# q and k of an attention unit: one transfer each over 128 partitions in place of two halves of 64

## The chip, the core and the metric

The kernel runs on one core of a Trainium2 chip. The metric is device time in microseconds for one execution of the whole program. The profile names the engines PE (matmul), PEld (weight load of the matmul engine), DVE (vector), ACT (scalar), POOL (GpSimd) and SP (the engine that mostly issues transfers). The core has 16 DMA engines, which move the data of every transfer, whichever engine issues it.

## What is computed

A decoder block with two parallel token mixers over 2048 positions of width 1024, batch 1. One combined projection gives q, k and v for 24 heads of 64 in three groups, gates, and the input of a recurrent branch. The attention branch is the part that matters here:

```python
for g, (window, dilation) in enumerate(((128, 1), (512, 4), (2048, 16))):
    o_g, lse_g = dilated_band_attention(q[:, :, g], k[:, :, g], v[:, :, g], window, dilation)
    outs.append(o_g)
    lses.append(lse_g)
wts = jax.nn.softmax(jnp.stack(lses, axis=0), axis=0)
attn = jnp.sum(wts[..., None] * jnp.stack(outs, axis=0), axis=0)
y_a = (attn.reshape(B, S, ATTN_OUT_WIDTH) * jax.nn.silu(g_attn)) @ w_attn_proj
...
merged = gates[:, :, 0] * y_a + gates[:, :, 1] * y_b
x = layer_norm(DEEPNORM_ALPHA * x + merged @ w_out + b_out, ln_gain, ln_bias)
```

Each query block of 128 sees its own key block and the one before it, along a residue class of the dilation.

## The kernel before

The program has three stages, one behind the other on PE, each engine working through a list that is fixed when the program is built.

**The projection** (L639) fills the first two thirds of the time. Its results go to DRAM: q and k after the rotary embedding into `qk_scr`, one buffer of 128 rows by 2048 float32 for each unit, v into `v_scr`, the rest into other scratch buffers. A row of `qk_scr` holds one head dimension of one of the unit's two heads, and rows of the two heads alternate.

**Attention** works on 12 units, each a pair of heads of one group. A unit has 16 query blocks and is done in four groups of the loop over `G`, 48 groups in all. In a group PE makes the scores of four blocks (`scores`, L992 and L998), turns the probabilities (`turn_p`, L1029), multiplies by v (`values`, L1061), and, from the fourth group on, does a piece of the second branch's output projection (`yb_part`, L1231). The scores of a unit read the tile `AT_X["qk", u % 2]`, 128 partitions by 2 by 2048: index 0 of the middle axis is q, 1 is k. Head 0 of the pair lies on partitions 0 to 63, head 1 on 64 to 127. There are two such tiles, so unit u + 1 is loaded while unit u is worked on, into the tile that unit u - 1 has left.

**The tail** does the rest of `yb`, the output projections and the layer norm.

The loads that the change touches are issued on SP's queue. `qk_parts(u)` (L791) gives a list of functions, each of which issues one load. Those of units 0 and 1 are called at steps 1 and 5 of the last pass of the projection (`begin`). For the others the loop at L1304 puts them into groups: the loads of q of unit u + 1 are issued in group 4u, the first group of unit u, those of k in group 4u + 1:

```python
for u in range(1, 11):
    for i, fn in enumerate(qk_parts(u + 1)):
        at_group(4 * u + i // 2, fn)
    for i, fn in enumerate(v_parts(u + 1)):
        at_group(4 * u + 1 + i // 2, fn)
```

Beside them SP issues, in the same stretch and in an order fixed by the code: the weights of `yb` (`wlr`, L1181), its inputs (`hx`, L1202), its gates (`gB`, L1215) and results (`yb_scr`, L1242), v (`V`, L815 to L819), and the softmax statistics (`ml_scr`, `mt`, L1085 to L1101; `wh`, L1148). Transfers issued on SP take eight completion semaphores in turn (DMAHW0 to DMAHW7 in the rows below), and each waits until the transfer eight places ahead of it, which had the same semaphore, has landed.

Of the kernel before, what the change touches and what calls it, by code (L numbers as in the profile page):

```python
# [31 lines left out]
def hybrid_block_kernel(ctx: ExitStack, tc: tile.TileContext, a: dict, out: bass.AP):  # L32
    nc = tc.nc
    sp, act, dve, pool, pe = nc.sync, nc.scalar, nc.vector, nc.gpsimd, nc.tensor
# [17 lines left out]
    qk_scr = {(n, u): dram.tile([P, S], F32, name=f"{n}_scr{u}") for u in range(12) for n in ("q", "k")}  # L52
# [53 lines left out]
    def big(slot, shape, dt, name):  # L106
        return (cur["Z"] if slot[0] == "Z" else X).tile(shape, dt, name=name, tag=slot)
# [203 lines left out]
    lo_, up_ = slice(0, 64), slice(64, P)  # L311
# [248 lines left out]
    qk = [("qk", FT_K + u, FT_Q + u) for u in range(12)]  # L560
# [152 lines left out]
    for s, pl in enumerate(plan):  # L713
        if pl[0] and pl[4] == "ug":
            i = pl[1][1][0] - FT_U
# [68 lines left out]
    AT_X = {}  # L784
    UG = {0: 0, 2: 1, 1: 2}

    def unit(u):

        return (0, 2, 1)[u % 3], u // 3

    def qk_parts(u):  # L791

        g, hp = unit(u)

        def part(x, h, hs):
            def fn():
                if u < 2 and (x, h) == (0, 0):
                    AT_X["qk", u] = big(("X2", "X3")[u], [P, 2, S], F32, f"qk{u}")
                src = qk_scr["qk"[x], 4 * g + hp].rearrange("(d h) s -> h d s", h=2)
                sp.dma_start(AT_X["qk", u % 2][hs, x], src[h])  # L800
            return fn

        return [part(x, h, hs) for x in range(2) for h, hs in ((0, lo_), (1, up_))]

    def v_parts(u):
        g, hp = unit(u)
        src = v_scr[g][hp]

        def part(i):
            def fn():  # L810
                if u == 0 and i == 0:
                    AT_X["v"] = big("X4", [P, 2, 16, P], F32, "V")
                V = AT_X["v"][:, u % 2, 4 * i:4 * i + 4]
                if g == 0:
                    sp.dma_start(V, src.rearrange("(p n) f -> p n f", p=P)[:, 4 * i:4 * i + 4])  # L815
                elif g == 1:
                    sp.dma_start(V, src[i * CH:(i + 1) * CH].rearrange("(j r) f -> j r f", r=4))
                else:
                    sp.dma_start(V, src.rearrange("(i r) f -> i r f", r=16)[:, 4 * i:4 * i + 4])  # L819
            return fn  # L820

        return [part(i) for i in range(4)]
# [48 lines left out]
    for t in sorted(early):  # L871
        for fn in early[t]:
            at(max(t, 0), fn)

    begin = {1: qk_parts(0), 3: v_parts(0), 5: qk_parts(1)}
    low = NS
    where = [(s, j) for s in range(NQ) for j in range(ticks[s])]
# [401 lines left out]
    def at_group(g, fn):  # L1279
        todo.setdefault(g, []).append(fn)  # L1280
# [22 lines left out]
        at_group((1, 1, 2, 2, 3, 3, 4, 4)[k], lambda k=k: split_h(k))  # L1303
    for u in range(1, 11):  # L1304
        for i, fn in enumerate(qk_parts(u + 1)):
            at_group(4 * u + i // 2, fn)
        for i, fn in enumerate(v_parts(u + 1)):
            at_group(4 * u + 1 + i // 2, fn)
    WS = {}
# [19 lines left out]
    for hp in range(3):  # L1329
        e = 4 * (3 * hp + 2) + 4  # L1330
        for i in range(12):
            c, g = i // 3, (0, 2, 1)[i % 3]
# [328 lines left out]
```

## Time and profile before

| | |
|---|---|
| median of 3 runs | 2112.81 us (2111.79 to 2115.16) |
| span of the profiled execution, first to last instruction | 2110.6 us |
| median of the runs less that span | 2.2 us |
| first and last matmul of scores start at | 1451.15 and 1764.4 us |
| loads of q and k | 48 of 512 KB |
| moved in the whole execution | 443.10 MB |

The profiled execution gives its span alone; what lies around it is taken as the 2.2 us in the table. In the profile a tile's name stands without its number, so `qk` is both tiles. Rows of a timeline give the start, the duration, the engine (with q where only its instruction queue is meant), the line, the operation with out<-in, and how many such instructions are merged. For a transfer the duration is that of issuing it, not of moving the data.

### The profile page before, as it was taken

Reading aid. Unit: us, or ns where it says so; the run is one execution under the profiler, and the core shown is the slowest. Engines: PE = TensorE matmul, PEld = TensorE weight load, DVE = VectorE, ACT = ScalarE, POOL = GpSimd, SP = SyncE. Lnnn points to the kernel's source line nnn. Section 1 sums busy time; section 2 is a strip of 40 time slices with the busy share of each in tenths; the row PEclk is TensorE's granted clock in tenths of the full one; section 3 lists DMA queues with packets and bytes.
Section 4 is the critical chain, followed back from the end, with each engine's and each line's share of the span. In section 5 each row is a group of like instructions: output and inputs, shape, how many; then the busy total and the mean of one; then the engine's idle time right before and its main releaser. Section 6 shows DMA issues by size and latency. Waiting matters only on the chain.

```text
span 2110.6 us, 35731 instructions
## 1 busy us (share of the span) xinstructions
PE 2092.4 (99%) x12069; PEld 1713.1 (81%) x12069; DVE 1645.0 (78%) x2937; ACT 1212.7 (57%) x2510; POOL 764.2 (36%) x685
## 2 busy tenths in 40 slices
PE   9999999999999999999999999999999999999998
PEld 7888888888888888888888888887888878788886
DVE  8878988989988868677777878875667776877667
ACT  6456556567567556677677787775666664321100
POOL 1544653653653301111111111112547678521120
PEclk9999999999999999999999999999999999999999
DMA  7876976886886866566665666669879886774431
GB/s 222 245 230 196 266 227 203 255 239 208 248 256 210 301 192 181 191 205 174 206 190 175 207 205 204 188 205 275 209 208 260 233 234 184 243 243 154 152 100 70
DMA packets 259205, 443.10 MB, mean 210 GB/s; under 512 B 65504, under 2 KB 92160, under 8 KB 255952
## 3 DMA queue, kind: packets, MB, share of 16 engines
q1 hardware_dynamic: 242384, 408.38, 62.0%
q0 software_dynamic: 11744, 23.54, 6.0%
q10 hardware_dynamic: 4896, 8.92, 1.1%
q8 instruction: 96, 1.57, 0.3%
q14 instruction: 85, 0.70, 0.1%
HBM read 289.74 MB, written 150.99 MB: 209 GB/s over the span
## 4 chain that ended last, share of the span: by engine, by line
PE 95%; DMA 2%; DVE 1%; POOL 1%; ACT 1%; issue 1%; SPq 0%; ACTq 0%; POOLq 0%; DVEq 0%
PE q L639 65%; PE yb L1231 6%; PE o L1061 3%; PE z L1536 3%; PE z L1537 3%; PE z L1538 3%; PE pt L1029 2%; PE s L998 2%; PE ya L1504 1%; PE ya L1503 1%; PE ya L1505 1%; PE g L500 1%; PE vtp L370 1%; PE s L992 1%; DMA war<-in_w_f_dram 1%
## 5 line engine op out<-in xcount | busy, mean ns | idle before, releaser
L639 PE MATMUL q<-xT,hS 128*128 128x512 f32 x1632 | 505.0, 391 | 0.1
L639 PE MATMUL q<-xT,l 128*128 128x512 f32 x1088 | 423.5, 389 | 0.0
L639 PE MATMUL q<-xB,hA 128*128 128x512 f32 x1344 | 418.0, 392 | 0.0
L639 PE MATMUL q<-xB,l 128*128 128x512 f32 x944 | 367.9, 390 | 0.0
L639 PEld LDWEIGHTS q<-xT,hS 128*128 128x128 f32 x1632 | 304.6, 188 | 65.0 <-issue 2.7
L639 PEld LDWEIGHTS q<-xB,hA 128*128 128x128 f32 x1344 | 250.7, 188 | 57.0 <-issue 5.8
L639 PEld LDWEIGHTS q<-xT,l 128*128 128x128 f32 x1088 | 204.3, 188 | 42.6
L240 POOL TENSOR_TENSOR sw<-sw,sin 128x512 f32<-128x512 f32 x96 | 156.8, 1639 | 166.2 <-ACT sw L329 94.7
L639 PEld LDWEIGHTS q<-xB,l 128*128 128x128 f32 x944 | 177.5, 188 | 37.2
L240 POOL TENSOR_TENSOR y<-y,h 128x512 f32<-128x512 f32 x28 | 38.8, 1386 | 384.1 <-DVE h L541 352.1
L1014 ACT ACTIVATE pb<-pb 128x192 f32<-128x192 f32 (+1 forms) x384 | 160.7, 422 | 26.5 <-DVE pb L1012 26.4
L639 PE MATMUL q<-xB,hS 128*128 128x512 f32 x544 | 169.0, 392 | 0.0
L639 PE MATMUL q<-xT,hA 128*128 128x512 f32 x544 | 167.8, 390 | 0.0
L284 ACT ACTIVATE hA<-wA 128x512 fp32r<-128x512 f32 x220 | 138.6, 636 | 28.5 <-DVE l L240 9.1
L1231 PE MATMUL yb<-hx,wl 128*128 128x512 f32 x576 | 148.9, 400 | 0.1
L284 ACT ACTIVATE hS<-S 128x512 fp32r<-128x512 f32 x170 | 108.6, 639 | 60.7 <-DVE S L240 47.3
L240 POOL TENSOR_TENSOR l<-wA,hA 128x512 fp32r<-128x512 f32 x68 | 107.8, 1585 | 91.4 <-ACT hA L284 60.9
L1231 PEld LDWEIGHTS yb<-hx,wl 128*128 128x128 f32 x576 | 104.8, 188 | 28.4 <-issue 5.6
L639 PEld LDWEIGHTS q<-xT,hA 128*128 128x128 f32 x544 | 101.9, 188 | 21.4 <-issue 0.4
L639 PEld LDWEIGHTS q<-xB,hS 128*128 128x128 f32 x544 | 101.2, 188 | 21.5 <-issue 1.1
L240 DVE TENSOR_TENSOR S<-S,wA 128x512 f32<-128x512 f32 x102 | 96.8, 949 | 11.5 <-DMA wA<-in_w_in_dram 7.9
L1507 POOL TENSOR_TENSOR me<-gA,me 128x512 f32<-128x512 f32 x30 | 47.7, 1607 | 157.6 <-DVE gA L1506 135.3
(213 smaller groups left out, 4325.4 us busy)
## 6 DMA issues: line engine op xcount, KB each, us to landing
wA<-in_w_in_dram SPq DMA_DIRECT2D x220, 256.0 KB
wl_scr<-l SPq DMA_DIRECT2D x102, 512.0 KB
l<-wl_scr SPq DMA_DIRECT2D x102, 512.0 KB
wS<-in_w_in_dram SPq DMA_DIRECT2D x102, 256.0 KB
wS<-in_w_in_dram POOLq DMA_DIRECT2D x68, 256.0 KB, 7.0
wlr<-in_w_f_dram SPq DMA_DIRECT2D x64, 256.0 KB
mg_scr<-y SPq DMA_DIRECT2D x59, 256.0 KB
v_scr<-vs SPq DMA_DIRECT2D x48, 256.0 KB
```

The source lines that it names most:

```text
L240: eng.tensor_tensor(out=out, in0=in0, in1=in1, op=op)
L284: act.activation(heads(h), heads(r, False), AF.Copy)
L639: pe.matmul(bank, w[:, ks], x[:, kk, xx], start=(first and i == 0), stop=(last and i == 11))
L998: pe.matmul(bank[h][es, b, 0:BW], q[hs, n * P + 64 * e:n * P + 64 * e + 64], k_[hs, at + 64 * e:at + 64 * e + BW], start=True, stop=True)
L1014: act.activation(pp, pp, AF.Exp, scale=-1.0, bias=mm, accum_out=ll)
L1029: pe.transpose(pt[e][:, b, 2 * h + x, :], pdata(p, h, c, c + P)[hs], ident[hs, hs])
L1061: pe.matmul(o[hs, 2 * i + b, :], V[:, kb, 64 * h:64 * h + 64], ptb[:, b, 2 * h + x, :], start=(x == lo // P), stop=(x == 1))
L1231: pe.matmul(YB["t"], w[:, a, k], hx(8 * c + k)[:, b], start=(hf == 0 and m == 0), stop=(hf == 1 and m == 11))
L1507: (dve if i in (6, 7) else pool).tensor_tensor(out=ME[c][:, f], in0=ga, in1=ME[c][:, f], op=ALU.add)
L1536: pe.matmul(z, mh[:, k], w[:, 0, hs], start=(k == 0), stop=False)
L1537: pe.matmul(z, mh[:, k], w[:, 1, hs], start=False, stop=False)
L1538: pe.matmul(z, ml[:, k], w[:, 0, hs], start=False, stop=(k == 7))
```

## The change

The list of `qk_parts` has two functions in place of four. Each issues one load whose destination is all 128 partitions of q or of k, and whose source is the whole buffer, seen as head, dimension, position. The view of the source is the one that was there before; it was cut at its first axis before and is passed whole now. The list being half as long, the loop's `i // 2` becomes `i`.

```diff
-        def part(x, h, hs):
+        def part(x):
             def fn():
-                if u < 2 and (x, h) == (0, 0):
+                if u < 2 and x == 0:
                     AT_X["qk", u] = big(("X2", "X3")[u], [P, 2, S], F32, f"qk{u}")
-                src = qk_scr["qk"[x], 4 * g + hp].rearrange("(d h) s -> h d s", h=2)
-                sp.dma_start(AT_X["qk", u % 2][hs, x], src[h])
+                sp.dma_start(AT_X["qk", u % 2][:, x], qk_scr["qk"[x], 4 * g + hp].rearrange("(d h) s -> h d s", h=2))
             return fn
 
-        return [part(x, h, hs) for x in range(2) for h, hs in ((0, lo_), (1, up_))]
+        return [part(x) for x in range(2)]
...
         for i, fn in enumerate(qk_parts(u + 1)):
-            at_group(4 * u + i // 2, fn)
+            at_group(4 * u + i, fn)
```

SP's list at the end of the projection, before: the loads of units 0 and 1, with v of unit 0 between them, and behind them the first weights and inputs of `yb`. A row gives the line, the operation, out<-in, the shape of the destination and a count.

```order
L800 DMA qk_13859<-q_scr_90 64x2048 x2
L800 DMA qk_13859<-k_scr_91 64x2048 x2
L815 DMA V<-v_scr_78 128x512 x4
L800 DMA qk_13937<-q_scr_106 64x2048 x2
L800 DMA qk_13937<-k_scr_107 64x2048 x2
L1181 DMA wlr_14029<-in_w_f_dram 128x512
L1181 DMA wlr_14030<-in_w_f_dram 128x512
L1202 DMA hx_13980<-hb_scr 128x512 x4
```

The same place in the changed program, here with the semaphores that each row waits for:

```order
L799 DMA qk_13859<-q_scr_90 128x1x2048 [waits DMAHW5_49,PE_49]
L799 DMA qk_13859<-k_scr_91 128x1x2048 [waits DMAHW6_49]
L814 DMA V<-v_scr_78 128x512 [waits DMAHW7_49,PE_49]
L814 DMA V<-v_scr_78 128x512 [waits DMAHW0_49]
L814 DMA V<-v_scr_78 128x512 [waits DMAHW1_49]
L814 DMA V<-v_scr_78 128x512 [waits DMAHW2_49]
L799 DMA qk_13935<-q_scr_106 128x1x2048 [waits DMAHW3_49]
L799 DMA qk_13935<-k_scr_107 128x1x2048 [waits DMAHW4_49]
L1180 DMA wlr_14025<-in_w_f_dram 128x512 [waits DMAHW5_49,PE_49]
L1180 DMA wlr_14026<-in_w_f_dram 128x512 [waits DMAHW6_49,Pool_49]
```

Eight rows of 64x2048 have become four of 128x1x2048; nothing else has changed its place, and the eight semaphores are reached again four transfers later. The first `wlr` now waits for the semaphore of the first load of q, the second for that of k.

The same inside attention, from the load of q of unit 3 to that of unit 4, before:

```order
L800 DMA qk_13937<-q_scr_92 64x2048 x2
L1181 DMA wlr_14852<-in_w_f_dram 128x512
L1181 DMA wlr_14853<-in_w_f_dram 128x512
L1085 DMA ml_scr_59<-mls_14846 64x128
L800 DMA qk_13937<-k_scr_93 64x2048 x2
L815 DMA V<-v_scr_79 128x512 x2
L1215 DMA gB_14947<-mg_scr 128x512
L1242 DMA yb_scr<-gB_14718 128x512
L815 DMA V<-v_scr_79 128x512 x2
```

and in the changed program, with the waits:

```order
L799 DMA qk_13935<-q_scr_92 128x1x2048 [waits DMAHW6_49,PE_49]
L1180 DMA wlr_14845<-in_w_f_dram 128x512 [waits DMAHW7_49,Pool_49]
L1180 DMA wlr_14846<-in_w_f_dram 128x512 [waits DMAHW0_49,Pool_49]
L1084 DMA ml_scr_59<-mls_14839 64x128 [waits DMAHW1_49,Activation_49]
L799 DMA qk_13935<-k_scr_93 128x1x2048 [waits DMAHW2_49]
L814 DMA V<-v_scr_79 128x512 [waits DMAHW3_49]
L814 DMA V<-v_scr_79 128x512 [waits DMAHW4_49,PE_49]
L1214 DMA gB_14939<-mg_scr 128x512 [waits DMAHW5_49]
L1241 DMA yb_scr<-gB_14712 128x512 [waits DMAHW6_49,DVE_49]
```

Here too only the pairs of rows became one row each. The `yb_scr` store, the fourth transfer behind k, waits for the semaphore of the load of q. On PE, DVE, ACT and POOL the lists hold the same instructions in the same order; what differs there is the semaphores that stand for the transfers.

## The prediction

> **What bounds the kernel now.** I read the page first: how busy each engine is.
>
> ```profile
> span 2110.6 us, 35731 instructions
> PE 2092.4 (99%) x12069; PEld 1713.1 (81%) x12069; DVE 1645.0 (78%) x2937; ACT 1212.7 (57%) x2510; POOL 764.2 (36%) x685
> ```
>
> PE has work in hand for all but 18 us. Then the list of PE's waits, which is short:
>
> ```profile
> PE first_bank L849 <- ACT warm L841: 3.2, 1, 3.2
> PE pt L1029 <- ACT ptb L1042: 2.3, 3, 1.5
> PE pt L1029 <- ACT pb L1014: 2.1, 2, 1.9
> PE mlt L1082 <- DVE o L1077: 0.6, 1, 0.6
> PE yb L1231 <- ACT wl L1192: 0.5, 1, 0.5
> ```
>
> No transfer stands in it: PE waits for engines alone, and little. The stage in which the change lies, attention, by stretches (length, then busy time of PE, PEld, DVE, ACT, POOL, the granted clock, the share of the DMA engines' time, GB/s):
>
> ```profile
> 1451.00:1471.00 20.00, 17.25 (x301) 13.62 (x302) 16.00 (x78) 16.73 (x67) 7.30 (x10) 0.91 1.01 319
> 1471.00:1743.00 272.00, 269.53 (x3441) 219.62 (x3438) 189.88 (x823) 182.43 (x758) 178.94 (x223) 1.00 0.86 229
> ```
>
> PE lacks 2.75 us of the first and 2.47 us of the second: **5.2 us is all that attention can gain**. But the DMA engines are at 0.86 of their time, so they are the next limit, with little room. The instructions that touch the tile `qk`:
>
> ```profile
> L998 PE MATMUL s<-qk x864: 322/323/524, 1451.6 to 1764.4; 64*64 64x192 f32 x173
> L992 PE MATMUL s<-qk x336: 272/272/373, 1451.2 to 1743.2; 64*128 64x128 f32 x168
> L800 SPq DMA_DIRECT2D qk<-q_scr x24: 450/506/1252, 1434.9 to 1717.5; - x24
> L800 SPq DMA_DIRECT2D qk<-k_scr x24: 444/588/1419, 1436.7 to 1726.6; - x24
> its engine sat idle before it (us, times) until:
>   issue: 0.4, 1
> ```
>
> The scores never wait for a load: the loads are hidden. When units 0, 1, 4 and 11 begin, from the timeline of PE (a unit's first blocks have no key block ahead of them, and so stand under L992):
>
> ```profile
> 1451.15 0.49 PE L992 MATMUL s<-qk 64*128 64x128 f32 x4
> ...
> 1471.28 0.99 PE L992 MATMUL s<-qk 64*128 64x128 f32 x13
> ...
> 1552.95 0.78 PE L992 MATMUL s<-qk 64*128 64x128 f32 x10
> ...
> 1742.40 1.11 PE L992 MATMUL s<-qk 64*128 64x128 f32 x16
> ```
>
> Unit 0, with no `yb` beside it, takes 20 us, units 1 to 10 take (1742.4 - 1471.3) / 10 = 27.1 us each. The loads of q and k in SP's timeline, of units 0, 1 and 5:
>
> ```profile
> 1434.93 1.74 SPq L800 DMA_DIRECT2D qk<-q_scr  x2
> 1436.73 1.23 SPq L800 DMA_DIRECT2D qk<-k_scr  x2
> 1442.20 1.55 SPq L800 DMA_DIRECT2D qk<-q_scr  x2
> 1445.69 3.42 SPq L800 DMA_DIRECT2D qk<-k_scr  x2
> ...
> 1553.65 1.15 SPq L800 DMA_DIRECT2D qk<-q_scr  x2
> 1560.53 1.23 SPq L800 DMA_DIRECT2D qk<-k_scr  x2
> ```
>
> The loads of unit 5 are issued 0.7 and 7.6 us after unit 4 begins (the tile is free only then), and have some 24 us until unit 5 needs them.
>
> **What is removed.** 24 issues of 0.45 to 1.4 us (the two rows above) leave SP's list; SP does no arithmetic and PE never waits for it, so they are worth nothing. The order of everything else stays, as the rows of the change show. So far the answer is no change. What decides is how the new transfer is moved.
>
> **What is added: a source whose outermost axis has two steps.** The view "h d s" has h = 2 outside. Before, h was cut off, and the outermost axis was 64 rows on both sides. How a transfer's shape decides who moves it is in no view, but the trace's semaphore records show it; I counted the updates that each transfer of this execution makes on its semaphore:
>
> ```
> L1101 mt<-ml_scr   source 8 x 4 x 32, destination 32 x 32    9 updates, each of 32 transfers
> L1148 wh<-w_scr    source 12 x 512,   destination 12 x 512  13 updates, each of 16 transfers
> L800  qk           source 64 x 2048,  destination 64 x 2048 16 updates, each of 48 transfers
> every other transfer, outermost axis 16 or more on both sides: 16 updates
> ```
>
> I read this as one update by each DMA engine that carries a share, and one more for the missing ones together: 8 + 1, 12 + 1, 16. The number of engines is then the outermost count that both sides can be cut into, at most 16, and L1101 shows that a source of 8 decides although its destination has 32 partitions. The new transfer is of L1101's kind, 2 x 64 x 2048 into 128: **it would go over two DMA engines**, one for each head, 512 KB for each.
>
> The Trainium skill, page "DMA: Bandwidth & Descriptors", says the same in "Rules for kernel authors" (the row on using all 16 engines) and in "Why a DMA increments its semaphore by 16 and not by 1": the slowest axis longer than 1 of both access patterns sets how many engines share a transfer. By that rule the change puts each load on two engines; the counts of 9 and 13 agree with it.
>
> **Price of one load.** No row shows one engine alone with 8 KB rows, so it is bounded. From the windows of the DMA queues (packets, MB, share of 16 engines) over 1872 to 1875, 1497 to 1503, and 1480 to 1750, in this order:
>
> ```profile
> q1 hardware_dynamic: 351, 1.25, 103.0%
> q1 hardware_dynamic: 324, 1.36, 94.0%
> q1 hardware_dynamic: 29624, 59.04, 82.2%
> ```
>
> The first is a stretch of 4 KB rows into 128 partitions: 1.25 MB / (3 us x 16 x 1.03) = 25.3 GB/s for a busy engine, so 524,288 B take 20.7 us. The second is almost only halves of q and k, 16 engines crowding into 64 partitions: 1.36 / (6 x 16 x 0.94) = 15.1 GB/s, 34.8 us. I take **20.7 us**: two engines, each writing 64 partitions of its own, are nearer to the uncrowded stretch.
>
> **What else these two engines carry.** All other transfers still put a sixteenth of their data on each of them, in the order of issue. The stretch 1480 to 1750 in whole and its loads of q and k:
>
> ```profile
> DMA packets 30503, 62.04 MB, mean 230 GB/s; under 512 B 7751, under 2 KB 8643, under 8 KB 28024
> qk<-k_scr SPq DMA_DIRECT2D x20, 512.0 KB
> qk<-q_scr SPq DMA_DIRECT2D x18, 512.0 KB
> ```
>
> 38 halves are 19.9 MB; 42.1 MB are left, 264 KB per engine in 27.1 us. At 25.3 GB/s that is 10.4 us. From the other side: q1's 82.2% of 270 us is 222 us per engine, and the halves at 15.1 GB/s take 82 us of it, so 140 us / 10 units = 14 us. I take 12.5 us.
>
> **The new period.** The loads of unit u + 1 can't begin before unit u - 1 is done with the tile, and unit u + 1 can't begin before both have landed. So one unit costs 2 x 20.7 + 12.5 + a gap. In the gap, from k's landing to the next q, SP must issue what stood behind k (its eighth successor waits for k's semaphore), while the two engines work off what was queued; before, q came from 0.7 us after its unit's start (above), and I estimate 2 us, with 0 to 5 as bounds. The period is 55.9 us in place of 27.1, far over PE's work, which then hides beside it. The wait lands on PE at the first scores of each unit; behind it in PE's list stand turns, values and `yb`, none of which can go ahead, and DVE, ACT and POOL run dry with it.
>
> **The sum.** Unit 0: 1434.93 + 2 x 20.7 + 2 for landing = 1478.3, against 1451.15. Unit 1: its loads queue behind those and v's 1 MB (64 KB per engine, 2.6 us): 1478.3 + 2.6 + 41.4 = 1522.3. Unit 11: 1522.3 + 10 x 55.9 = 2081.3, against 1742.4, so 338.9 us later. From there on no q or k is loaded, and the remaining 368.2 us (2110.6 - 1742.4) stay. Span 2110.6 + 338.9 = 2449.5; with the 2.2 us by which the median of the runs exceeds this span, **2452 us**.
>
> **Rivals.**
> *All 16 engines move it after all.* Then 1 MB takes 1,048,576 / 16 / 25.3 GB/s = 2.6 us of each engine, hidden as before, and the result lies between 2112.8 and 2112.8 - 5.2 = 2107.6 us, not slower. It decides if the split goes by the 128 partitions of the destination. For it: the destination alone would allow it. Against it: L1101, where 32 partitions gave 9 updates. The Trainium skill, page "DMA: Bandwidth & Descriptors", section "Rules for kernel authors", in its row on transfers to disjoint partition halves, advises one 128-partition transfer, as both halves share the same engines; by that row alone the result would be this one. The trace bears the sharing out (16 updates for each half), but the row doesn't speak of a source cut in two. Chance 6%.
> *Two engines, at the crowded rate.* 34.8 us per load: period 69.6 + 14 + 2 = 85.6; unit 0 at 1506.5, unit 1 at 1578.7, unit 11 at 2434.7, 692 us late: 2805 us. For it: it is the only row with 8 KB rows. Against it: there sixteen engines shared 64 partitions. Chance 8%.
> *A split over four engines*, were the axes cut otherwise: 10.4 us per load, period 20.8 + 12.5 + 2 = 35.3; unit 0 at 1457.7, unit 1 at 1481.1, unit 11 at 1834, 92 us late: 2204 us. Nothing in the counts speaks for it. Chance 4%.
> That the change doesn't do what it says is excluded by the rows of the order: 24 transfers of 128x1x2048 in place of 48.
>
> **How the numbers follow.** The forecast holds 80%. Its own bounds: low, a period of 41.4 + 10.4 + 0 = 51.8, unit 11 at 1522.3 + 518 = 2040.3, giving 2411; I set 2400, as two engines alone might be a little over 25.3 GB/s. High: the page's mean of this queue is 408.38 MB in 62.0% of 16 x 2110.6 us,
>
> ```profile
> q1 hardware_dynamic: 242384, 408.38, 62.0%
> ```
>
> or 19.5 GB/s and 26.9 us per load; with 14 and 5 the period is 72.8, unit 1 at 1547.1, unit 11 at 2275.1, giving 2645 us. The range is 2400 to 2650; the rivals lie outside it with 18% and the rest, 2%, anywhere. A difference under 0.2%, about 4 us, can't be told from none by measurement. Slower by more: 80 + 8 + 4 + 2 = 94%. Of the first rival's 6%, its span of 5.2 us lies mostly within 0.2%: same 4.5%, faster 1.5%.
>
> **What would show it.** Right: PE waits at L991 (the scores' line, moved up by one) or in `pt` behind it, for `qk`, some 25 to 30 us at the start of nearly every unit, PE's busy share of attention near a half, units about 56 us apart, GB/s there falling to about 230 x 27.1 / 55.9 = 112, the granted clock dipping after each wait, and the tail unchanged at some 368 us. A period near 86 says the crowded rate; 35, four engines; no waits at all, sixteen. The forecast is wrong in its core if the new loads' semaphores show 16 updates and not 3.

## The result and the profile after

| | before | changed |
|---|---|---|
| median, run side by side | 2112.3 us (2111.36 to 2115.16, 4 runs) | 2457.49 us (2456.95 to 2459.85, 4 runs) |
| ratio, 95% interval | | 1.1631, 1.1614 to 1.1647 |
| span of the profiled execution | 2110.6 us | 2455.0 us |

The change makes the kernel 16.3% slower; 2452 us had been forecast. The page of the changed kernel, its first lines and the slices of the span:

```profile
span 2455.0 us, 35689 instructions
...
PE 2137.6 (87%) x12069; PEld 1744.5 (71%) x12069; DVE 1646.3 (67%) x2937; ACT 1212.0 (49%) x2510; POOL 764.2 (31%) x685
...
PE   9999999999999999999999964665454654999998
...
PEclk9999999999999999999999986787777777999999
...
DMA  7778768778786557566665552323333333676441
...
PE 75%; DMA 21%; DVE 1%; issue 1%; POOL 1%; ACT 1%; SPq 1%; ACTq 0%; DVEq 0%; POOLq 0%
```

The first 23 slices and the last six are as busy on PE as ever. Between them lies attention, where PE falls to about half and the DMA engines, far from being overrun, to a third. The last line is the chain that ended last: 21% of the span, some 515 us, is transfers. The stretches of attention and of the tail, in the columns of the windows shown before:

```profile
1481.00:2085.00 604.00, 331.78 (x3726) 265.07 (x3728) 202.83 (x895) 197.82 (x822) 185.08 (x230) 0.74 0.34 113
2085.00:2455.00 370.00, 359.06 (x1856) 294.30 (x1854) 269.90 (x471) 80.25 (x177) 118.09 (x102) 0.99 0.49 163
```

PE is busy for 331.78 / 604 = 55% of attention, at a granted clock of 0.74, and the DMA engines for 0.34 of their time, where it was 0.86. When units 0, 1, 2, 3 and 11 begin, from PE's timeline; the bracket is the idle time ahead of the row and what ended it:

```profile
1481.19 0.80 PE L991 MATMUL s<-qk 64*128 64x128 f32 x4 [31.14 <-DMA qk<-k_scr]
...
1526.42 0.98 PE L991 MATMUL s<-qk 64*128 64x128 f32 x5 [26.71 <-DMA qk<-k_scr]
...
1580.81 1.44 PE L991 MATMUL s<-qk 64*128 64x128 f32 x10 [19.69 <-DMA qk<-k_scr]
...
1630.95 0.80 PE L991 MATMUL s<-qk 64*128 64x128 f32 x4 [19.43 <-DMA qk<-k_scr]
...
2084.71 1.48 PE L991 MATMUL s<-qk 64*128 64x128 f32 x16
```

Each of the first units begins when its k has landed. The period is (2084.71 - 1526.42) / 10 = 55.8 us, against 27.1 before. Unit 11 begins 342.3 us later than before (1742.4), which is all of the difference but 2.1 us. PE's waits in the whole execution (total, times, longest):

```profile
PE s L991 <- DMA qk<-k_scr: 163.0, 8, 31.1
PE w L1154 <- DMA wh<-w_scr: 79.7, 3, 29.8
PE pt L1028 <- DVE ptb L1043: 19.2, 6, 8.1
PE s L991 <- issue: 13.0, 1, 13.0
```

The first row is the wait that the prediction named. The second it did not name: three times, ahead of units 5, 8 and 11, PE waits for `wh`, the weights of the softmax over the groups. That the loads go over two engines is seen between 1488 and 1498 us, where hardly anything but loads of q and k moves; the queue's row there:

```profile
q1 hardware_dynamic: 64, 0.52, 12.5%
```

64 packets of 8 KB in 10 us, and the share of the 16 engines is 12.5%, which is exactly two engines, busy all the time: 0.52 MB / 10 us / 2 = 26 GB/s each. The records of the semaphores say the same: each of the 24 loads makes 3 updates, two engines and one for the missing ones, where each half made 16.

### The profile page after: what moved, and what is told of

Same layout as the page of the kernel before. It is cut to its first block, busy times and chain, and to the rows that moved or that the text cites. A ratio compares the mean times of both kernels' runs of the same rounds, so it can differ in the third digit from the quotient of the medians.

```text
span 2455.0 us, 35689 instructions
## 1 busy us (share of the span) xinstructions
PE 2137.6 (87%) x12069; PEld 1744.5 (71%) x12069; DVE 1646.3 (67%) x2937; ACT 1212.0 (49%) x2510; POOL 764.2 (31%) x685
## 4 chain that ended last, share of the span: by engine, by line
PE 75%; DMA 21%; DVE 1%; issue 1%; POOL 1%; ACT 1%; SPq 1%; ACTq 0%; DVEq 0%; POOLq 0%
PE q L639 56%; DMA qk<-k_scr 9%; DMA V<-v_scr 5%; PE yb L1230 3%; PE z L1537 2%; PE z L1536 2%; PE z L1535 2%; DMA ga<-ga_scr 2%; PE o L1060 2%; DMA gB<-mg_scr 1%; DMA hx<-hb_scr 1%; PE ya L1503 1%; PE ya L1504 1%; PE ya L1502 1%; PE g L500 1%
## 5 line engine op out<-in xcount | busy, mean ns | idle before, releaser
L991 PE MATMUL s<-qk 64*128 64x128 f32 x336 | 32.8, 346 | 176.0 <-DMA qk<-k_scr 163.0
L1230 PE MATMUL yb<-hx,wl 128*128 128x512 f32 x576 | 159.9, 418 | 16.5 <-POOL hx L1205 12.7
L991 PEld LDWEIGHTS s<-qk 64*128 64x128 f32 x336 | 28.4, 247 | 177.3 <-issue 137.9
L1230 PEld LDWEIGHTS yb<-hx,wl 128*128 128x128 f32 x576 | 110.0, 198 | 50.7 <-POOL hx L1205 13.7
L1041 ACT ACTIVATE ptb<-pt 128x512 f32<-128x512 f32 (+2 forms) x120 | 55.0, 479 | 142.1 <-PE pt L1028 142.1
```

The source lines that it names most:

```text
L991: pe.matmul(bank[h][:, b, lo:256], q[hs, n * P:(n + 1) * P], k, start=True, stop=True)
L1041: act.activation(dst, src, AF.Copy)
L1230: pe.matmul(YB["t"], w[:, a, k], hx(8 * c + k)[:, b], start=(hf == 0 and m == 0), stop=(hf == 1 and m == 11))
```

## Experiments

Times are medians; the ratio is to the kernel before, run beside it. The period is that of units 1 to 11, (start of unit 11 - start of unit 1) / 10, and the updates are those that a load of q and k makes on its semaphore, counted in the trace's records.

| run | loads of q and k | updates | period, us | time, us | ratio (95%) |
|---|---|---|---|---|---|
| before | 48 halves | 16 | 27.1 | 2112.3 | 1 |
| the change | 24, outermost axis 2 | 3 | 55.8 | 2457.5 | 1.1631 (1.1614 to 1.1647) |
| e1 | 48 halves, outermost axis 2 | 3 | 59.1 | 2485.6 | 1.1767 (1.1749 to 1.1785) |
| e2 | 48 halves, outermost axis 4 | 5 | 41.8 | 2280.8 | 1.0805 (1.0785 to 1.0824) |
| e5 | 48 halves, outermost axis 8 | 9 | 32.1 | 2173.2 | 1.0278 (1.0263 to 1.0294) |
| e4 | q as in the change, k in halves | 3, 16 | 42.0 | 2293.1 | 1.0857 (1.0842 to 1.0872) |
| e3 | 16 in one piece, 8 as two halves | 16 | 27.1 | 2112.5 | 1.0000 (0.9991 to 1.0008) |
| e9 | 24, outermost axis 128 | 16 | 27.1 | 2111.8 | 0.9991 (0.9982 to 1.0) |
| e6 | the change, `wh` on another queue | 3 | 54.5 | 2453.1 | 1.1606 (1.1587 to 1.1626) |
| e7 | the change, on ACT's queue | 3 | 57.3 | 2475.7 | 1.1712 (1.1695 to 1.1729) |
| e8 | the change, k issued with q | 3 | 57.0 | 2468.6 | 1.1679 (1.1662 to 1.1696) |

**Is it the outermost axis or the one wide transfer?** Three kernels take the two apart. In e1 the halves of before stay as they are, 64 partitions, two for each tile; only the view of the source has its 64 rows cut into 2 times 32:

```diff
-                src = qk_scr["qk"[x], 4 * g + hp].rearrange("(d h) s -> h d s", h=2)
+                src = qk_scr["qk"[x], 4 * g + hp].rearrange("(d y h) s -> h y d s", h=2, y=2)
                 sp.dma_start(AT_X["qk", u % 2][hs, x], src[h])
```

> The 48 halves of before stay, 64 partitions each, but each half's source is read as 2 x 32 rows instead of 64 (the same reordering of a head's dimensions for q and for k, so the scores are the same). Theory A (the outermost axis of the source sets how many DMA engines carry a transfer): each half goes over two engines, 256 KB per engine and half, so a unit's q and k still put 1 MB on each of two engines, as in the change: about 2457 us, 3 updates on the semaphore of each half, units some 56 us apart. Theory B (the loss comes from one transfer filling all 128 partitions, or from there being 24 transfers in place of 48): no loss, 2108 to 2117 us.

The rows of a head go to the same 64 partitions as before, in another order, the same for q and for k, and the kernel takes 2485.6 us. In PE's waits and at units 1 and 11 in its timeline:

```profile
PE s L992 <- DMA qk<-k_scr: 173.6, 16, 27.1
```

```profile
1523.06 0.76 PE L992 MATMUL s<-qk 64*128 64x128 f32 x2 [15.93 <-DMA qk<-k_scr]
...
2114.12 1.11 PE L992 MATMUL s<-qk 64*128 64x128 f32 x16
```

So the whole loss comes without the wide transfer, from a 2 at the outside of the source's view. It is not that the new order makes the rows slow: the median row of 8 KB takes 311 ns in e1, and took 594 before. Theory A's 2457 us is missed by 28: of the 3.3 us by which a unit is longer than in the change, about 2 are rows (mean 340 ns in place of 324), and the rest stays open. In e9 the wide transfer stays and the 2 goes: the source is taken as 128 rows in their stored order. This leaves out the sorting by head, so its scores mix the two heads; it is a kernel for the time alone.

```diff
-sp.dma_start(AT_X["qk", u % 2][:, x], qk_scr["qk"[x], 4 * g + hp].rearrange("(d h) s -> h d s", h=2))
+sp.dma_start(AT_X["qk", u % 2][:, x], qk_scr["qk"[x], 4 * g + hp])
```

> The change with the view of the source taken away: 24 loads of 128 partitions, the source read as 128 rows in the order in which they lie. The rows then stand in the wrong partitions (the sorting by head is left out, so the scores mix the two heads); every instruction and every byte is as in the change. Theory A (the view's outermost axis of two is the whole loss): 16 updates for each load, no wait of PE for qk, 8 KB rows near 0.31 us throughout, 2107 to 2114 us, so the difference to the change, some 345 us, is the view alone, and one transfer in place of two brings nothing. Theory B (part of the loss is in the merged transfers): between 2130 and 2457 us. Were the freed issues and the faster rows worth something, it would be 2107 to 2109 us, the 5 us that PE lacks in attention.

2111.8 us, at the edge of what can be told from before (0.9982 to 1.0). The windows of attention in e9, beside those of before:

```profile
1451.00:1471.00 20.00, 17.34 (x318) 13.83 (x312) 16.46 (x79) 17.71 (x71) 15.48 (x18) 0.91 0.85 304
1471.00:1743.00 272.00, 270.08 (x3448) 220.06 (x3444) 189.63 (x835) 182.47 (x759) 172.21 (x217) 1.00 0.68 224
```

PE is as busy as before (270.08 against 269.53 of 272 us), but the DMA engines need 0.68 of their time in place of 0.86 for nearly the same data. e3 reaches the wide source in another way, with the heads kept apart: the stores of q and k put a unit's two heads one behind the other where the layout of the group allows it (q of groups 0 and 1, k of groups 0 and 2), so that 16 of the 24 tiles come in one transfer; the other 8 come as halves.

```diff
+        by_h = dst.rearrange("(h d) s -> d h s", h=2)
...
-            sp.dma_start(dst[:, c * CH:(c + 1) * CH], flat(rp))
+            sp.dma_start(by_h[:, :, c * CH:(c + 1) * CH], flat(rp))
...
-                sp.dma_start(AT_X["qk", u % 2][:, x], qk_scr["qk"[x], 4 * g + hp].rearrange("(d h) s -> h d s", h=2))
+                src = qk_scr["qk"[x], 4 * g + hp]
+                if g != (2, 1)[x]:
+                    sp.dma_start(AT_X["qk", u % 2][:, x], src)
+                    return
...
```

> One transfer over 128 partitions stays where the rows of a buffer can be stored head by head (q and k of group 0, k of group 2, q of group 1: 16 of the 24 loads), its source being 128 rows; the other 8 are halves as before. The stores of those buffers write 64 x 2 rows instead of 128. Theory A: 16 engines, 16 updates, no wait of PE for qk; 2107 to 2114 us, at best the 5 us that PE lacks in attention; 8 KB rows of the whole loads near 0.31 us, those of halves near 0.6. Theory B: 16 of 24 loads keep the loss, about 2112 + 16/24 x 345 = 2340 us.

The time is that of before, within 0.1%. The window of units 1 to 10 shows what was saved:

```profile
1471.00:1743.00 272.00, 270.00 (x3454) 220.13 (x3450) 189.82 (x826) 182.56 (x758) 175.21 (x220) 1.00 0.73 225
```

The DMA share falls from 0.86 to 0.73, and nobody had waited for it. The Trainium skill, page "DMA: Bandwidth & Descriptors", section "Rules for kernel authors", advises one transfer over 128 partitions in place of two halves; e3 and e9 follow it and gain at most 0.2%.

**How the loss follows the number of engines.** e2 and e5 are e1 with 4 and 8 in place of 2:

```diff
-                src = qk_scr["qk"[x], 4 * g + hp].rearrange("(d y h) s -> h y d s", h=2, y=2)
+                src = qk_scr["qk"[x], 4 * g + hp].rearrange("(d y h) s -> h y d s", h=2, y=4)
```

> As the halves on two engines, but the source read as 4 x 16 rows. Theory A: four engines, 512 KB of q and k per engine and unit, 64 rows at 0.311 us = 19.9 us in place of 39.8; with the other 16 us of the change's period (55.8 - 39.8) the period is 36, unit 11 some 90 us later than before: about 2200 us (2150 to 2215, less if the 16 us shrink where PE's own 27 us get near), 5 updates for each half. Theory B: 2108 to 2117 us.

The counts are 5 and 9, which is 4 + 1 and 8 + 1, so the number of engines was foreseen rightly. The Trainium skill, page "DMA: Bandwidth & Descriptors", section "Why a DMA increments its semaphore by 16 and not by 1", lets the slowest axis of both sides set that number, and these counts agree. The time of e2, 2280.8 us, lies far over the 2150 to 2215 that were expected. From its timeline, units 1 and 11, and its waits:

```profile
1488.85 0.46 PE L992 MATMUL s<-qk 64*128 64x128 f32 x2 [0.68 <-DMA qk<-k_scr]
...
1906.81 1.46 PE L992 MATMUL s<-qk 64*128 64x128 f32 x16
```

```profile
PE w L1155 <- DMA wh<-w_scr: 46.8, 3, 17.3
PE s L992 <- DMA qk<-k_scr: 44.4, 11, 13.4
```

The period is 41.8 us, not 36, and more than half of these two waits is again the wait for `wh`. e4 halves the loss in another way: q as in the change, k in halves over 16 engines.

```diff
-        return [part(x) for x in range(2)]
+        def half(h, hs):
+            src = qk_scr["k", 4 * g + hp].rearrange("(d h) s -> h d s", h=2)
+            return lambda: sp.dma_start(AT_X["qk", u % 2][hs, 1], src[h])
+
+        return [part(0)] + [half(h, hs) for h, hs in ((0, lo_), (1, up_))]
...
-            at_group(4 * u + i, fn)
+            at_group(4 * u + (i + 1) // 2, fn)
```

> The change for q alone; k in two halves as before. Theory A: a unit has one narrow load, 19.9 us on two engines, with about 3.5 us for the halves of k and 7 to 16 us for the rest: period 31 to 39 in place of 55.8 and of 27.1, 2160 to 2240 us. Rival (the loss is a fixed delay of each narrow load, which the 27 us of a unit's work cover as long as one is late): about 2112 us. Theory B: about half the loss, 2285 us.

2293.1 us, over the 2160 to 2240 of theory A and near theory B's 2285, which is half of the change's loss: the run shows 180.1 us over before, of 345.2. Theory B itself is ruled out by e1 and e9; what was wrong is A's sum, a period of 31 to 39 us where the run shows 42.0. The waits:

```profile
PE s L995 <- DMA qk<-k_scr: 37.9, 10, 15.6
PE w L1158 <- DMA wh<-w_scr: 31.3, 3, 14.7
PE pt L1032 <- DVE ptb L1047: 31.0, 5, 13.3
```

The wait for k is there although k goes over 16 engines. The two engines that carry q also carry a sixteenth of k, and it lands behind q: in unit 2, k is issued at 1513.7 us while q is under way and lands 24.0 us later, 4.8 us after q; in unit 10, where q has landed before k is issued, k needs 10.0 us. What was still open was whether other work hides below PE's 27 us once the narrow loads are short. e5 asks that with eight engines, where the rows of a unit's loads take only 128 x 0.311 x 2 / 8 = 10.0 us of an engine, at 311 ns for a row alone.

```diff
-                src = qk_scr["qk"[x], 4 * g + hp].rearrange("(d y h) s -> h y d s", h=2, y=2)
+                src = qk_scr["qk"[x], 4 * g + hp].rearrange("(d y h) s -> h y d s", h=2, y=8)
```

> As the halves on two and on four engines, but the source read as 8 x 8 rows: 9 updates for each half, 32 rows of 0.311 us = 10.0 us per unit on each of eight engines. The periods so far are 27.1 us (16 engines), 41.8 (four engines, 19.9 us of rows), 59.1 (two, 39.8 us). If each engine adds its rows to a fixed rest, the line through the last two gives 33 us here and 2112 + 6 x 10 + 5 = about 2175 us. If only engine time beyond PE's 27 us counts (10.0 + 12.5 us of the rest = 22.5 us, less than 27.1), the loss is a few us: 2112 to 2125 us.

It hides in some units and not in others: 2173.2 us, period 32.1 us.

```profile
1477.22 0.44 PE L992 MATMUL s<-qk 64*128 64x128 f32 x2
...
1797.91 1.33 PE L992 MATMUL s<-qk 64*128 64x128 f32 x16
```

```profile
PE w L1155 <- DMA wh<-w_scr: 18.5, 3, 8.2
...
PE s L992 <- DMA qk<-k_scr: 5.2, 2, 3.3
```

```profile
1477.00:1798.00 321.00, 286.81 (x3432) 230.43 (x3426) 189.16 (x822) 181.98 (x757) 185.22 (x230) 0.93 0.73 203
```

The starts of the units in PE's timeline show where the time goes. Units 2 and 3 take 26.9 and 30.2 us, to a tenth what they took before; of the 49.6 us that units 1 to 10 are longer, 44.8 stand in units 1, 4, 7 and 10, which were the four shortest before (24.3 to 26.1 us). PE hardly waits for q or k any more: k has landed 3 to 10 us ahead of the unit's start in eight of units 2 to 11. What is left is for the most part the wait for `wh` (18.5 us) and PE's own work: PE is busy for 286.81 us in these units against 269.53 before, at a granted clock of 0.93 in place of 1.00, so some 17 us of the loss are PE's own work taking longer.

Taking from each period the time of a unit's rows at 311 ns leaves:

```
            period   rows of q and k per engine    rest
change      55.8     128 x 0.311      = 39.8       16.0
e1          59.1     128 x 0.311      = 39.8       19.3
e2          41.8     128 x 0.311 / 2  = 19.9       21.9
e5          32.1     128 x 0.311 / 4  = 10.0       22.1
```

The 311 ns are right for the rows on two engines alone. With more engines in 64 partitions the rows get slower: in units 2 to 11 their mean is 324 ns in the change, 340 in e1, 403 in e2 and 487 in e5 (median 460; 478 over all loads). So 5.9 us of e2's rest are rows, which is what e2's period has over the expected 36. For e5 the last column is an average over units in which the loads hide and units in which they do not, and no rest that the rows add to. The wait for `wh` is tied to k: SP holds the load of `wh` back for the semaphore of k, 34.6 us in e2 and 12.6 in e5. What `wh` on another queue is worth there was not tried.

**What is in the rest of the change's period?** From the semaphore records and PE's starts, over units 2 to 11: from the issue of q to the landing of k 48.5 us (44.7 to 52.0), of which 39.8 are rows; from the landing of k to the unit's start at most 0.1 us in seven of the ten, but 7.6, 8.0 and 9.3 in units 5, 8 and 11, 2.6 in the mean; from the unit's start to the next q 4.8 us in the mean. Together they are the period. Units 5, 8 and 11 are those ahead of which PE waits for `wh`.

Both small terms come from SP's list. A transfer eight places behind k waits for k's semaphore, and SP stands still until then: these waits come to 95.0 us in units 1 to 11, three of them (21.9 us) at the load of `wh`. Within 0.3 us of k's landing SP goes on, and issues 4 to 17 transfers before it comes to the next q. The tile is not what holds q back: the scores that read it last have ended 27 to 41 us before. In e6 the load of `wh` leaves SP's queue:

```diff
-        sp.dma_start(flat(WH[c % 2][32 * (c // 2):32 * (c // 2) + 12]), w_scr[hp][:, c * CH:(c + 1) * CH])
+        pool.dma_start(flat(WH[c % 2][32 * (c // 2):32 * (c // 2) + 12]), w_scr[hp][:, c * CH:(c + 1) * CH])
```

> The change, but the twelve small loads of the softmax weights (wh, 24 KB each, units 4, 7 and 10) are issued by POOL on its own queue instead of SP. In the change units 4, 7 and 10 take 63.2, 63.5 and 62.2 us, and PE waits 79.7 us for wh. Theory Q (small loads stand in line behind the 1 MB of the load of k on the same queue, and the work of the unit that needs them is done only after k has landed): these units fall to some 52 us, 33 us in all, about 2424 us. Rival (k's landing sets the period whatever stands before it on PE): 2450 to 2460 us, PE then waiting for k as much longer.

```profile
PE s L991 <- DMA qk<-k_scr: 223.7, 11, 31.6
...
PE w L1154 <- DMA wh<-w_scr: 4.2, 2, 4.0
```

2453.1 us, as the rival reading had it. The wait for `wh` falls from 79.7 to 4.2 us, and the wait for k grows from 163.0 to 223.7: 60.7 of the 75.5 us come back in it. The period falls by 1.3 us, the tail grows by 5.5, and the kernel takes 4.4 us less. The wait for `wh` stood in front of a wait for k that was there anyway.

e7 and e8 ask whether it is the order of the queue that costs, SP issuing k late and others behind it. e7 issues the loads on ACT's queue, where no SP transfer stands ahead of them:

```diff
-                sp.dma_start(AT_X["qk", u % 2][:, x], ...
+                act.dma_start(AT_X["qk", u % 2][:, x], ...
```

> The change, but the loads of q and k are issued by ACT on its own queue; they stay on two engines (3 updates). Theory Q: the other transfers no longer stand in line behind them, the engine takes from both queues in turn; the two engines still have 39.8 us of rows and 7 to 12.5 us of the rest in each unit, so 47 to 52 us per unit: 2360 to 2410 us. Rival (the engines' time alone, order without effect): 2445 to 2465 us. Rival 2 (what is lost is lost in SP's blocked queue, not in the engines): near 2112 us.

```profile
PE s L991 <- DMA qk<-k_scr: 231.0, 12, 34.6
PE pt L1028 <- ACT ptb L1041: 63.8, 7, 22.8
PE w L1154 <- DMA wh<-w_scr: 35.8, 2, 18.9
```

All 12 units now begin at a wait for k, `wh` is waited for less, and the kernel is 18 us slower than the change, above all three readings. The row in the middle has grown from 10.9 us: PE waits for ACT. In four of the seven waits, 58.6 of the 63.8 us, PE goes on 1.0 to 1.3 us after ACT has issued a unit's k, so ACT stood in its own list until then. The Trainium skill, page "DMA: Bandwidth & Descriptors", section "Rules for kernel authors", says that spreading transfers over the issuing engines doesn't help bandwidth, as all of them use the same DMA engines; this run agrees. e8 issues k right behind q:

```diff
-            at_group(4 * u + i, fn)
+            at_group(4 * u, fn)
```

> The change, but the load of k is issued in the same group as that of q, right behind it, instead of one group later. In the change k is issued 7 to 11 us after q and lands some 47 us after q's issue, with rows of other transfers between the two. If the two engines' time sets the period, only what stood between them moves behind: 2440 to 2465 us. If the late issue of k costs its 7 to 11 us per unit: 10 x 9 = 90 us less, about 2370 us.

```profile
PE s L991 <- DMA qk<-k_scr: 136.2, 6, 31.5
PE pt L1028 <- DVE ptb L1043: 87.9, 6, 29.0
PE w L1154 <- DMA wh<-w_scr: 53.3, 2, 28.6
```

From the issue of q to the landing of k it is now 45.7 to 48.0 us in units 2 to 11, a little less. But in units 5 and 7 to 11 the unit begins 8.5 to 11.6 us after k's landing, as other transfers come late instead: DVE waits 115.6 us for the gates `gB`, in place of 49.1. The time of the two engines is shared out otherwise, and with 2468.6 us the sum is no smaller. None of these three changes of queue and order gives the time back; more engines do. Not tried was to issue q earlier: the 7.3 us from k's landing to the next q are set by SP's list, while the tile is free. No kernel here is faster than before by more than 0.2%.

## Why the prediction came out right

- **What is removed is worth nothing.** Right: e9 has the same 24 issues fewer and is within 0.2% of before. The price of the change is not in SP's list.
- **Two engines carry each load.** Right: 3 updates for each load, 12.5% of the 16 engines in the window of loads alone, and e1, where the 2 in the source's view alone makes the loss. The counts of 9 and 13 in the trace of before were read as they had to be; axes of 2, 4 and 8 gave 3, 5 and 9.
- **20.7 us per load.** The median row of 8 KB takes 311 ns in the changed kernel, so 64 of them 19.9 us, and the mean 324 ns, or 20.7 us: the value taken, that of the uncrowded stretch, is between 4% high and exact. The stretch read as "almost only halves of q and k" had 1.04 of its 1.36 MB in rows of 8 KB; they alone moved at 14.0 GB/s, so the rival's price was rather too low. The crowded rate, the rival of 2805 us, would have been 544 ns; before, the same rows took 594 ns with sixteen engines in 64 partitions, in e9 309 ns with sixteen in 128.
- **12.5 us for what else the two engines carry, and a gap of 2 us.** Both mis-sized, against each other; that they cancel is luck. What stands beside the rows between q's issue and k's landing is 48.5 - 39.8 = 8.7 us, below the bound of 10.4. The gap is 2.6 + 4.8 = 7.3 us (7.33 before rounding), above the bound of 5. Its reason was right, SP issuing what stands behind k, whose eighth successor waits for k; but there are 4 to 17 such transfers, and `wh` among them holds PE ahead of three units. The sum of the period, 55.9, stands against 55.8 measured, but 1.6 us too much for the rows and 3.8 for the others (0.1 and 5.5 by the mean of the rows) were made up by 5.3 too little for the gap.
- **"The tile is free only then."** The reading is wrong, and with it the reason given why one unit's loads come behind the other's. Before, the scores of unit 3 end at 1547.0 us, 6.7 us ahead of the loads of unit 5; in the change a tile is free for 27 to 41 us before its q is issued. That they come one behind the other holds, through SP's list and not through the tile, so the form of the sum stands.
- **The path to unit 11.** Unit 0 began at 1481.19 us (forecast 1478.3), unit 1 at 1526.42 (1522.3), unit 11 at 2084.71 (2081.3). Of the 5.5 us by which the span was put too short, 4.1 are there at unit 1, ten periods take 0.7 back, and the tail adds 2.1.
- **The tail stays.** 2455.0 - 2084.71 = 370.3 us, against 368.2.
- **What the profile would show.** PE's share near a half: 55%. GB/s about 112: 113. The clock dipping: 0.74. A wait of 25 to 30 us at nearly every unit's start: eight waits with 163.0 us, 20 us in the mean, so both number and size were put too high, as three units were held by `wh` ahead of their start and one start stands under "issue" (13.0 us).
- **The rival of sixteen engines**, 2107.6 to 2112.8 us, is e9, at 2111.8. **The rival of four engines** gave 2204 us; e2, which puts the loads on four, takes 2280.8. The same sum that fits at two engines is off by 6.5 us a period there: 5.0 for the rows, 25.8 us at their mean of 403 ns in place of 20.8, and 1.5 for all else, 16.0 in place of 12.5 + 2.

## What to carry to other kernels

Before two transfers are merged, look at the outermost axis that the merged one has on each side: here a 2 there put 1 MB per unit on each of two of the sixteen engines and cost 345 us, while the same transfer with 128 outside cost nothing. To have 128 there, the rows must lie in DRAM in the order of the partitions, as the stores of e3 put them for 16 of the 24 loads; e9 shows only the time. The count of a transfer's semaphore updates in a trace of the kernel as it is tells how many engines a shape gets, before anything is run. A low DMA share (0.34) beside an engine waiting for transfers meant few engines at work here, not a free path. And a list of transfers that share a few semaphores passes a late one on: here every transfer from the eighth behind k on stood until k had landed.

## What was not expected of the hardware

The issue of a transfer, 0.4 us in SP's list, grew to many microseconds where narrow loads were under way. Before and after, the loads of v for the units of group 0 (min, median and max in ns):

```profile
L815 SPq DMA_DIRECT2D V<-v_scr x16: 322/384/691, 1440.4 to 1672.6; - x16
```

```profile
L814 SPq DMA_DIRECT2D V<-v_scr x16: 432/2868/19857, 1439.2 to 1951.8; - x16
```

And in SP's timeline after, around the loads of units 0 and 1:

```profile
1433.77 0.64 SPq L799 DMA_DIRECT2D qk<-q_scr  x1
1434.46 0.54 SPq L799 DMA_DIRECT2D qk<-k_scr  x1
1439.20 21.79 SPq L814 DMA_DIRECT2D V<-v_scr  x4
1461.04 7.97 SPq L799 DMA_DIRECT2D qk<-q_scr  x1
1469.06 11.30 SPq L799 DMA_DIRECT2D qk<-k_scr  x1
```

Four loads of v take 21.79 us to issue, until q of unit 0 has landed (1460.4 us by its semaphore), and k of unit 1 only ends its issue at 1480.4, near the landing of k of unit 0 (1481.1). So while narrow loads are under way the issuing engine is held up too, and with it every transfer behind them in its list. What holds it up was not tried.

The other surprise is the row of 8 KB: 594 ns with sixteen engines writing 64 partitions, 309 ns with sixteen writing 128 (e9). These are medians; in the mean over units 2 to 11 it is 590 and 386 ns, so merging the halves in the right way takes a third off the engines' time for these loads. This kernel has no use for it.
